# One shared inverse root for several output rows, and an early scaling of the second half's scan output in a free place

## The chip, the cores and the metric

The kernel runs on one core of a Trainium2 chip. The metric is the device time of one execution in microseconds (us); three runs of the kernel before gave 2174.93, 2175.2 and 2177.97 us, with a median of 2175.2 us.

## The reference

One decoder block over 1024 tokens of width 1024, all in float32. What matters here is the middle and the end: the scan branch ends in a norm over groups of 512 channels and a projection, the two branches are merged by gates, the merge is projected and added to the residual, and after the feed-forward network the residual is normed once more.

```python
y = ssd_chunked(xs, dt, A, Bm, Cm) + d_skip[:, None] * xs
y = y.reshape(b, S, 2048) * silu(z)
yg = y.reshape(b, S, 4, 512)
yg = yg * rsqrt(mean(yg * yg, -1) + EPS)          # one factor per token and group
y_ssm = (yg.reshape(b, S, 2048) * ssm_norm) @ w_ssm_out
...
mixed = gates[:, :, 0] * y_ssm + gates[:, :, 1] * y_att
x = x + mixed @ w_mix_out
h = rmsnorm(x, norm_ffn)
x = x + (silu(h @ w_ffn_gate) * (h @ w_ffn_up)) @ w_ffn_down
return rmsnorm(x, norm_final)
```

## The kernel before

A float32 product is made of three passes of a faster format: each operand is split into a high part (a cast on ScalarE) and a low part (operand minus high part, on VectorE), and `mm3` issues high x high, high x low and low x high. TensorE therefore needs, for every weight tile and every activation tile, one cast and one subtraction done before it.

The program is written out by a planner. `Pace` keeps a modelled clock `pace.t`, which advances with the matmuls that are issued. Everything else runs in generator tasks: a task that yields a list waits until the modelled time at which those buffers are written, a task that yields a string waits for an event, a number is a delay. The tasks fix the order of instructions in each engine's queue; on the chip each engine works through its queue in that order and waits on semaphores. All DMAs are issued from SyncE's queue (SP).

SBUF buffers are pieces of 4 KB per partition ("slabs") in a store; `slabs.room(n)` waits until n are free. `wts` is the store for weights: `w_dma` loads a raw weight tile, `w_split` makes the high and low tiles, `pump` (called by `tick` between matmuls) does both ahead of use as far as free pieces allow. `N_WTS` and `N_WTS_B` set how many pieces it has.

The stages that the change touches, in order:

- **Input projection.** The normalised rows `hhi`, `hlo` (both token halves in one tile each, 2 x 8 x 512) are the moving operands. After the last gate unit they are not read again.
- **Merge stage, first token half (`th` 0), then second (`th` 1).** `y_load` fetches the scan output of one half from DRAM in eight pieces `kk` (two 128-row blocks each) and two attention pieces, and per two pieces the norm's factor of each token, spread over partitions (`yscale`). `y_task` multiplies a piece by that factor on GpSimd (L1678), then casts it on ScalarE with the channel weight (L1689) and subtracts on VectorE (L1693), and fires `y{th}{kk}`. `mx_unit` (L1815) runs eight units of 60 matmuls over the pieces; `mx_task` (L1760) gates the result and writes it, split, into the half `th` 1 of `h2hi`, `h2lo`. Then `mix_unit` (L1845) multiplies by `w_mix_out` in two column blocks `cb`, four weight tiles `kp` each, and `mo_task` (L1775) adds the residual, forms the norm and writes the transposed rows of this half into `h2`. For `th` 0, `y_load(1)` and `y_task(1)` are started at the last unit (L1881), so that the second half's pieces are scaled and split while TensorE is in `mix_unit` of the first half. `lend` gives `W_MIX` slabs to `wts` for that time, `give_back` returns them.
- **End.** The down projection runs in seven products `PRODUCTS`; `down_out` (L2123) adds each result to the residual rows `xr`. When a half row (`b`) of one of the eight row tiles `jj` is complete, `out_half` (L2101) squares it on ScalarE with an accumulated sum and multiplies it by the norm's weight on GpSimd (L2108). With the second half row done, `inverse_root` (L2086) computes one row tile's factor on VectorE, 12 instructions on 128x1 operands, each of which needs the one before; then ScalarE scales the right half, VectorE the left half, and two DMAs write 256 KB each. Of `jj` 4 to 7 the left half (`b` 0) is the last to be done; it comes with the last product, one row tile after the other.

## Time and profile before

| | |
|---|---|
| median of 3 runs | 2175.2 us |
| the profiled execution | 2177.34 us |
| its span, first to last instruction | 2175.6 us |
| its mean granted TensorE clock | 0.993 |
| TensorE busy | 2129.2 us (98%) |
| VectorE busy | 1552.6 us (71%) |
| ScalarE busy | 907.9 us (42%) |
| GpSimd busy | 648.9 us (30%) |

TensorE is busy almost throughout, so a change in another engine's work moves the time only where TensorE waits for it, or where TensorE has already finished. Busy shares of the other engines are means over stages and say little; what counts is the few stretches in which TensorE has fewer matmuls than its full rate. Times in the rows below are us from the span's start. "DVE" is VectorE, "ACT" ScalarE, "POOL" GpSimd, "SPq" the queue of DMA issues, "PEld" the weight load of TensorE. All instructions carry the line of one helper (L169), so they are told apart by the names of their buffers; the number behind a name says which use of the buffer it is.

### The profile page before, as it was taken

What the parts mean: (1) busy time and instruction counts of PE and PEld (TensorE: products, weight loads), DVE (VectorE), ACT (ScalarE), POOL (GpSimd) and SP (SyncE); (2) the same over time, 40 slices, a digit from 0 to 9 for tenths busy, and PEclk for the clock granted to TensorE, in tenths of its full rate; (3) what the DMA queues carried; (4) which work ended last, traced back from release to release, by engine and by line L of the source; (5) the groups of instructions that cost most, each with busy time, mean ns of one, the idle gap of its engine ahead of it and who ended that gap; (6) DMA issues with size and microseconds to landing.
All of it is one profiled execution on the core that took longest, in us unless ns stands there. A gap on an engine that the chain in (4) does not pass through costs nothing. (4 is left out here: it accounts for less than half of the span.)

```text
span 2175.6 us, 27860 instructions
## 1 busy us (share of the span) xinstructions
PE 2129.2 (98%) x10356; PEld 1758.6 (81%) x10356; DVE 1552.6 (71%) x2124; ACT 907.9 (42%) x1642; POOL 648.9 (30%) x420
## 2 busy tenths in 40 slices
PE   6999999999999999999999999999999999999996
PEld 6788878888887888788888887888888888888885
DVE  6697887866656787897854347644897777767787
ACT  4543444344355565455533224322433332324444
POOL 1233222332114454454431004001254444420002
PEclk9999999999999999999999999999999999999998
DMA  3533343434364556675486467364143323349332
GB/s 129 167 97 107 106 126 103 119 104 126 102 206 158 176 190 200 214 233 172 128 259 210 133 195 235 118 187 131 41 139 99 111 82 116 107 161 356 98 97 102
DMA packets 308939, 322.90 MB, mean 148 GB/s; under 512 B 20740, under 2 KB 246980, under 8 KB 308548
## 3 DMA queue, kind: packets, MB, share of 16 engines
q1 hardware_dynamic: 308804, 321.13, 46.5%
q8 instruction: 81, 1.33, 0.3%
q14 instruction: 54, 0.44, 0.1%
HBM read 236.54 MB, written 84.54 MB: 148 GB/s over the span
## 5 line engine op out<-in xcount | busy, mean ns | idle before, releaser
L169 POOL TENSOR_TENSOR xr<-xr,nfin 128x512 f32<-128x512 f32 x16 | 21.8, 1369 | 185.1 <-ACT jk L169 185.1
L169 POOL TENSOR_TENSOR slab__8_12293<-h2hi,h2lo 128x1024 f32<-128x1024 f32 x1 | 2.7, 2723 | 117.5 <-PE wide__54_11935 L169 117.5
L169 POOL TENSOR_TENSOR slab__29_10800<-slab__29_10800,last__1_10783 128x1024 f32<-128x1024 f32 x1 | 2.4, 2391 | 115.8 <-DMA slab__29_10800<-yt_d 115.8
L169 POOL TENSOR_TENSOR slab__3_5034<-slab__3_5034,slab__3_5032 128x1024 f32<-128x1024 f32 x1 | 2.4, 2391 | 69.1 <-DMA slab__3_5032<-in_rope 69.1
L169 ACT ACTIVATE jk<-xr 128x512 f32<-128x512 f32 x16 | 10.1, 632 | 15.4 <-DVE xr L169 11.2
L169 POOL TENSOR_TENSOR slab__61_12556<-more__4_12496 128x512 f32<-128x512 f32 x1 | 1.3, 1290 | 49.8 <-DMA more__4_12496<-in_w_ffn_up 49.8
L169 POOL TENSOR_TENSOR slab__2_644<-slab__2_642 128x512 f32<-128x512 f32 x1 | 3.8, 3784 | 37.8 <-DMA slab__2_642<-in_w_in 37.8
L169 PE MATMUL wide__1_208<-hhi,slab__1_272 128*128 128x256 f32 (+1 forms) x24 | 8.8, 365 | 2.7 <-ACT hhi L169 2.7
L169 PE MATMUL wide__1_208<-hlo,slab__1_272 128*128 128x256 f32 (+1 forms) x24 | 8.9, 370 | 2.3 <-DVE hlo L169 2.3
L169 POOL TENSOR_TENSOR slab__16_12681<-slab__18_12618 128x512 f32<-128x512 f32 x1 | 2.8, 2823 | 27.6 <-DVE slab__15_12627 L169 27.6
L169 POOL TENSOR_TENSOR slab__45_15700<-slab__29_15392,slab__60_15513 128x512 f32<-128x512 f32 x1 | 1.3, 1300 | 32.1 <-DVE slab__60_15513 L169 32.1
L169 POOL TENSOR_TENSOR slab__14_10033<-slab__14_10033,slab__10_9841 128x1024 f32<-128x1024 f32 x1 | 3.0, 2978 | 26.2 <-DMA slab__14_10033<-yt_d 26.2
L169 POOL TENSOR_TENSOR slab__1_620<-hhi,hlo 128x1024 f32<-128x1024 f32 x1 | 2.4, 2407 | 26.9 <-DVE hlo L169 26.9
L169 ACT ACTIVATE xr<-xr,or 128x512 f32<-128x512 f32 x8 | 5.6, 717 | 11.3 <-DVE or L169 11.3
L169 DVE TENSOR_TENSOR hlo<-slab__1_624,hhi 128x1024 fp32r<-128x1024 f32 x1 | 1.2, 1224 | 11.8 <-DMA slab__3_906<-in_w_in 11.8
L169 DVE TENSOR_TENSOR slab__22_5025<-slab__19_4802,slab__19_5024 128x1024 fp32r<-128x1024 f32 x1 | 1.2, 1224 | 11.5 <-issue 11.5
L169 PE MATMUL wide__35_7344<-hhi,slab__25_7221 128*128 128x512 f32 x16 | 6.9, 431 | 1.7 <-DVE slab__6_7342 L169 1.7
L169 PE MATMUL bank__1_210<-ident 128*128 128x128 f32 x36 | 5.9, 343 | 2.7 <-DMA ident<-in_consts 2.7
L169 POOL TENSOR_TENSOR slab__9_9508<-slab__9_9508,slab__4_9506 128x1024 f32<-128x1024 f32 x1 | 2.4, 2403 | 20.0 <-DMA slab__9_9508<-yt_d 20.0
L169 PEld LDWEIGHTS wide__1_208<-hlo,slab__1_272 128*128 128x128 f32 x24 | 5.2, 217 | 3.9 <-DVE hlo L169 3.8
L169 PEld LDWEIGHTS wide__1_208<-hhi,slab__1_272 128*128 128x128 f32 x24 | 5.1, 213 | 4.0 <-ACT hhi L169 3.8
L169 PE MATMUL wide__1_208<-hhi,slab__1_273 128*128 128x256 f32 (+1 forms) x24 | 8.2, 343 | 0.0
(7956 smaller groups left out, 8285.8 us busy)
## 6 DMA issues: line engine op xcount, KB each, us to landing
xr<-x_d SPq DMA_DIRECT2D x8, 512.0 KB, 6.7
out<-xr SPq DMA_DIRECT2D x16, 256.0 KB, 2.4
b_d<-hhi SPq DMA_DIRECT2D x1, 1024.0 KB, 5.2
b_d<-hlo SPq DMA_DIRECT2D x1, 1024.0 KB, 7.3
slab__1_174<-in_x SPq DMA_DIRECT2D x1, 512.0 KB, 3.3
slab__1_175<-in_x SPq DMA_DIRECT2D x1, 512.0 KB, 4.9
slab__1_182<-in_norm_mix SPq DMA_DIRECT2D x1, 512.0 KB
slab__1_189<-in_w_in SPq DMA_DIRECT2D x1, 512.0 KB
```

The source lines that it names most:

```text
L169: r = call(*args, **kw)
```

## The change

Three things are changed.

- The factor multiplication of the second half's scan pieces is taken out of `y_load(1)`/`y_task(1)`. A new task `y1_scaled`, started when the last gate unit has been issued, loads the eight pieces into the place of the first half of `hhi`/`hlo`, one every 7 us of modelled time or later, and multiplies them on GpSimd there. To that end `hhi`, `hlo`, `h2hi` and `h2lo` become one tile per half; the first half of `h2` gets its place only when the pieces have been split (`yield "y17"` in `mo_task`). `y_task(1)` starts its splits after `mx07`, that is when the last unit of the first half has been gated.
- The weight store has 9 pieces instead of 7 in the merge stage, and borrows 1 slab instead of 4.
- At the end the sums of squares go to three groups of row tiles, 0 to 3, 4 alone, and 5 to 7, with one inverse root each on 128x4, 128x1 and 128x3 operands. The root has 14 instructions instead of 12. For `jj` above 3 and `b` 0 the norm's weight is no longer multiplied on GpSimd but in VectorE's final scaling.

The diff without the lines that only follow from the split of `hhi`, `hlo` and `h2` into halves:

```diff
-K_PAD, R_PAD = 40, 24
+K_PAD, R_PAD = 72, 24
...
-W_MIX = 4
+W_MIX = 1
...
+N_WTS_M = 9
...
+    def scale_rows(g, th, place):
+        yield from place.room()
+        t = yscale[th, g] = place.get([P, 512])
+        nc.sync.dma_start(t.v, rs_d[g].rearrange("c l -> (c l)")[th * 512:(th + 1) * 512].partition_broadcast(P))
+
+    def by_rows(raw, kk, th):
+        rsb = yscale[th, kk // 2]
+        yield [rsb, raw]
+        nc.gpsimd.tensor_tensor(raw.v, raw.v, rsb.v.unsqueeze(1).to_broadcast([P, 2, 512]), ALU.mult)
+        if kk % 2:
+            rsb.free()
+
+    def fetch_y(raw, kk, th):
+        g, f0 = kk // 2, (kk % 2) * 2
+        for i in range(2):
+            nc.sync.dma_start(raw.v[:, :, i * 256:(i + 1) * 256], yt_d[g][2 * th + i][:, f0:f0 + 2, :])
+
+    def y1_scaled():
+
+        for kk in range(8):
+            yield 7.0
+            yraw[1, kk] = Part(y1[kk // 4][:, kk % 4])
+            if kk % 2 == 0:
+                yield from scale_rows(kk // 2, 1, halves)
+            fetch_y(yraw[1, kk], kk, 1)
+            yield from by_rows(yraw[1, kk], kk, 1)
+            pace.fire(f"yr1{kk}")
+
     def y_load(th):
         ts_ = slice(th * 512, (th + 1) * 512)
-        for kk in range(10):
+        for kk in range(8 * th, 10):
...
     def y_task(th):
+        if th:
+            yield "mx07"
         for kk in range(10):
             yield f"yr{th}{kk}"
             raw = yraw[th, kk]
             yield [raw]
-            if kk < 8:
-                rsb = yscale[th, kk // 2]
-                yield [rsb]
-                nc.gpsimd.tensor_tensor(raw.v, raw.v, rsb.v.unsqueeze(1).to_broadcast([P, 2, 512]), ALU.mult)
-                if kk % 2:
-                    rsb.free()
+            if kk < 8 and th == 0:
+                yield from by_rows(raw, kk, th)
...
-    wts.pieces.extend(slabs.pieces.popleft() for _ in range(N_WTS - N_WTS_B))
+    wts.pieces.extend(slabs.pieces.popleft() for _ in range(N_WTS_M - N_WTS_B))
...
         if cb == 0:
             return
+        if th == 0:
+            yield "y17"
+            for n in ("hi", "lo"):
+                h2[n][0] = hp.tile([P, KD, 512], F32R, tag=f"h{n}0", name=f"h2{n}0")
...
-    h2["hi"] = hp.tile([P, 2, KD, 512], F32R, tag="hhi", name="h2hi")
-    h2["lo"] = hp.tile([P, 2, KD, 512], F32R, tag="hlo", name="h2lo")
+    y1 = [hp.tile([P, 4, 2, 512], F32, tag=f"h{n}0", name=f"y1{n}") for n in ("hi", "lo")]
+    for n in ("hi", "lo"):
+        h2[n] = [None, hp.tile([P, KD, 512], F32R, tag=f"h{n}1", name=f"h2{n}1")]
+    pace.spawn(y1_scaled(), 0.0, 1)
...
-    def inverse_root(v, r, t, sq):
-        nc.vector.tensor_scalar(v, sq[:, 0:1], sq[:, 1:2], D * EPS, ALU.add, ALU.add)
+    def inverse_root(v, r, t, h, sq):
+        nc.vector.tensor_tensor(v, sq[:, :, 0], sq[:, :, 1], ALU.add)
+        yield v
+        nc.vector.tensor_scalar(v, v, EPS, None, ALU.add)
         yield v
         nc.vector.tensor_scalar(t.bitcast(I32), v.bitcast(I32), 1, None, ALU.logical_shift_right)
+        nc.vector.tensor_scalar(h, v, -0.5, None, ALU.mult)
         yield t
         nc.vector.tensor_scalar(r.bitcast(I32), t.bitcast(I32), -1.0, 1597463007.0, ALU.mult, ALU.add)
         yield r
-        for c in (1.0, 1.0, D ** 0.5):
-            nc.vector.scalar_tensor_tensor(t, r, v, r, ALU.mult, ALU.mult)
+        for _ in range(3):
+            nc.vector.tensor_tensor(t, r, h, ALU.mult)
             yield t
-            nc.vector.tensor_scalar(t, t, -0.5 * c, 1.5 * c, ALU.mult, ALU.add)
+            nc.vector.tensor_tensor(t, t, r, ALU.mult)
             yield t
-            nc.vector.tensor_tensor(r, r, t, ALU.mult)
+            nc.vector.scalar_tensor_tensor(r, t, 1.5, r, ALU.add, ALU.mult)
             yield r
 
     def out_half(jj, b):
-        first = jj not in sums
-        if first:
-            sums[jj] = small("osq", 2)
+
+        group, n = ((0, 4), (4, 1), (5, 3))[(jj > 3) + (jj > 4)]
+        i = jj - group
+        if group not in sums:
+            sums[group] = [small("osq", 8)[:, :2 * n].rearrange("p (n b) -> p n b", b=2), 2 * n]
+        s = sums[group]
+        late = jj > 3 and b == 0
         xj = xr[:, jj, b * 512:(b + 1) * 512]
         yield [xr]
-        nc.scalar.activation(jk[:, b * 512:(b + 1) * 512], xj, AF.Square, accum_out=sums[jj][:, b:b + 1])
-        nc.gpsimd.tensor_tensor(xj, xj, nfin[:, b * 512:(b + 1) * 512], ALU.mult)
-        if first:
+        nc.scalar.activation(jk[:, b * 512:(b + 1) * 512], xj, AF.Square, scale=D ** -0.5, accum_out=s[0][:, i, b:b + 1])
+        if not late:
+            nc.gpsimd.tensor_tensor(xj, xj, nfin[:, b * 512:(b + 1) * 512], ALU.mult)
+        s[1] -= 1
+        if s[1]:
             return
-        v, r, t = (small(n, 1) for n in ("ov", "or", "ot"))
-        yield [sums[jj]]
-        for w in inverse_root(v, r, t, sums[jj]):
+        v, r, t, h = (small(k, 4)[:, :n] for k in ("rv", "rs", "rt", "sq"))
+        yield [s[0]]
+        for w in inverse_root(v, r, t, h, s[0]):
             if jj < 4:
                 yield [w]
-        xj = xr[:, jj, :]
-        rows = slice(jj * P, (jj + 1) * P)
-        nc.scalar.activation(xj[:, 512:], xj[:, 512:], AF.Copy, scale=r)
-        nc.vector.tensor_scalar(xj[:, :512], xj[:, :512], r, None, ALU.mult)
-        nc.sync.dma_start(out[rows, :512], xj[:, :512])
-        nc.sync.dma_start(out[rows, 512:], xj[:, 512:])
+        for i in range(n):
+            rows = slice((group + i) * P, (group + i + 1) * P)
+            xj, ri = xr[:, group + i, :], r[:, i:i + 1]
+            nc.scalar.activation(xj[:, 512:], xj[:, 512:], AF.Copy, scale=ri)
+            if late:
+                nc.vector.scalar_tensor_tensor(xj[:, :512], xj[:, :512], ri, nfin[:, :512], ALU.mult, ALU.mult)
+            else:
+                nc.vector.tensor_scalar(xj[:, :512], xj[:, :512], ri, None, ALU.mult)
+            nc.sync.dma_start(out[rows, :512], xj[:, :512])
+            nc.sync.dma_start(out[rows, 512:], xj[:, 512:])
```

## Rows read from the trace of the kernel before

**Rows 1.** The table by stage, in stretches of 50 us. Columns: the stretch and its length, busy us and instructions (x) of PE, PEld, DVE, ACT and POOL, granted clock of TensorE as a share of full speed, busy share of the DMA engines, GB/s.

```profile
1250.00:1300.00 50.00, 50.00 (x222) 41.40 (x221) 19.52 (x25) 11.84 (x14) 0.00 (x0) 1.00 0.61 188
1300.00:1350.00 50.00, 46.59 (x199) 38.08 (x198) 40.60 (x35) 23.55 (x36) 21.87 (x8) 0.97 0.74 246
```

**Rows 2.** The same table over three stretches cut at the stages' own borders: the eight units of the first half, the last stretch with matmuls, and what follows the last matmul.

```profile
1203.00:1311.70 108.70, 108.70 (x482) 90.02 (x481) 43.12 (x52) 27.86 (x36) 4.88 (x3) 1.00 0.57 176
...
2100.00:2159.00 59.00, 58.50 (x256) 47.45 (x254) 49.69 (x122) 28.66 (x59) 13.33 (x11) 1.00 0.24 76
2159.00:2175.60 16.60, 0.03 (x1) 0.00 (x0) 10.11 (x44) 4.11 (x7) 2.37 (x2) 0.64 0.47 176
```

**Rows 3.** The waits of TensorE: what it was about to write, what released it; total us, times, longest.

```profile
PE bank__136_10900 L169 <- DVE slab__34_10952 L169: 3.4, 1, 3.4
...
PE bank__170_17092 L169 <- DVE slab__43_17287 L169: 0.5, 1, 0.5
```

**Rows 4.** The timeline of TensorE around that longest wait: the first matmul of the first half's mix, the last matmul ahead of the wait, and the one behind it (start us, us).

```profile
1311.69 0.39 PE L169 MATMUL bank__136_10900<-slab__27_10854,h2hi 128*128 128x512 f32 x1
...
1322.57 0.39 PE L169 MATMUL bank__136_10900<-slab__46_10951,h2hi 128*128 128x512 f32 x1
1326.37 0.50 PE L169 MATMUL bank__136_10900<-slab__34_10952,h2hi 128*128 128x512 f32 x1 [3.41 <-DVE slab__34_10952 L169]
```

**Rows 5.** The table by stage over the time right behind that wait (columns as in rows 1).

```profile
1326.37:1333.35 6.98, 6.98 (x24) 5.59 (x25) 6.89 (x6) 3.20 (x4) 2.19 (x1) 0.76 0.01 2
```

**Rows 6.** The timeline of VectorE in the same stretch: the subtractions of the second half's scan pieces (two SBUF inputs and "par"), the gating of the last unit (slab__10, input from PSUM in the first row of it), the weight subtraction that TensorE waits for (slab__34_10952), and a scan piece's subtraction later on.

```profile
1309.27 5.70 DVE L169 SCALAR_TENSOR_TENSOR slab__36_10850<-slab__29_10800,par,slab__35_10849 128x512 fp32r<-128x512 f32 x2 [3.33 <-ACT slab__35_10849 L169]
...
1316.03 1.27 DVE L169 SCALAR_TENSOR_TENSOR slab__10_10723<-slab__10_10723,wide__49_10782 128x512 f32<-128x512 f32 x2
1317.34 1.58 DVE L169 TENSOR_TENSOR slab__10_10723<-slab__10_10723 128x512 f32<-128x512 f32 x1
1318.85 3.56 DVE L169 SCALAR_TENSOR_TENSOR slab__14_10887<-slab__29_10812,par,slab__11_10886 128x512 fp32r<-128x512 f32 x2
1322.33 2.85 DVE L169 TENSOR_TENSOR h2lo<-slab__10_10723,h2hi 128x512 fp32r<-128x512 f32 x1
1325.10 1.21 DVE L169 TENSOR_TENSOR slab__34_10952<-slab__38_10837,slab__46_10951 128x1024 fp32r<-128x1024 f32 x1
...
1332.14 1.41 DVE L169 SCALAR_TENSOR_TENSOR slab__12_10978<-slab__28_10879,par,slab__29_10977 128x512 fp32r<-128x512 f32 x2
```

**Rows 7.** The timeline of GpSimd there: three of the eight multiplications of the second half's scan pieces.

```profile
1306.09 2.39 POOL L169 TENSOR_TENSOR slab__29_10800<-slab__29_10800,last__1_10783 128x1024 f32<-128x1024 f32 x1 [115.79 <-DMA slab__29_10800<-yt_d]
...
1315.56 2.82 POOL L169 TENSOR_TENSOR slab__28_10879<-slab__28_10879,last__1_10815 128x1024 f32<-128x1024 f32 x1 [1.14 <-DMA slab__28_10879<-yt_d]
...
1321.96 2.67 POOL L169 TENSOR_TENSOR slab__3_10979<-slab__3_10979,last__2_10932 128x1024 f32<-128x1024 f32 x1
```

**Rows 8.** The timeline of ScalarE and SP there: the cast of the weight tile that TensorE waits for, and the DMA issues of that tile and of the first scan piece of the second half.

```profile
1319.48 1.05 ACT L169 CAST slab__46_10951<-slab__38_10837 128x1024 fp32r<-128x1024 f32 x1
```

```profile
1299.83 0.75 SPq L169 DMA_DIRECT2D slab__29_10800<-yt_d  x1
...
1304.60 0.48 SPq L169 DMA_DIRECT2D slab__38_10837<-in_w_mix_out  x1
```

**Rows 9.** The chain that ended last, one piece of it: the first unit of the second half.

```profile
1360.88 13.94 PE wide__50_11248 L169 x60
```

**Rows 10.** The timelines at the border between the last two units of the first half: VectorE's low part of the last unit's first weight tile, and of its second; TensorE's first matmul of that unit, and its first one with that low part.

```profile
1295.80 1.23 DVE L169 TENSOR_TENSOR slab__45_10771<-slab__45_10736,slab__45_10770 128x1024 fp32r<-128x1024 f32 x1 [6.76 <-ACT slab__45_10770 L169]
...
1300.22 1.22 DVE L169 TENSOR_TENSOR slab__45_10795<-slab__37_10762,slab__46_10794 128x1024 fp32r<-128x1024 f32 x1
```

```profile
1298.09 0.39 PE L169 MATMUL wide__49_10782<-slab__26_9568,slab__45_10770 128*128 128x512 f32 x1
...
1298.54 0.39 PE L169 MATMUL wide__49_10782<-slab__26_9568,slab__45_10771 128*128 128x512 f32 x1
```

**Rows 11.** The timeline of the end: the last addition to the residual, the last square and the read of its sum, a root that starts (ov) and the scaling that follows it, and the last scalings of ScalarE and VectorE.

```profile
2159.06 0.69 DVE L169 SCALAR_TENSOR_TENSOR xr<-bank__181_17095,xr 128x512 f32<-128x512 f32 x1 [1.18 <-PE bank__181_17095 L169]
...
2160.39 0.18 ACT L169 ACTIVATION_READ_ACCUMULATOR jk<-xr 128x1 f32 x1
...
2164.16 0.21 DVE L169 TENSOR_SCALAR ov<-osq 128x1 f32<-128x1 f32 x1
...
2166.76 0.48 DVE L169 TENSOR_SCALAR xr<-xr,or 128x512 f32<-128x512 f32 x1
...
2169.82 1.33 ACT L169 ACTIVATE xr<-xr,or 128x512 f32<-128x512 f32 x2 [2.35 <-DVE or L169]
2169.83 0.88 DVE L169 TENSOR_SCALAR xr<-xr,or 128x512 f32<-128x512 f32 x2
```

**Rows 12.** VectorE from 2100 to 2176, grouped by operation and form (count | busy us, mean ns): the longest of the roots' small instructions, the final scaling, and an addition that has, as the new final scaling has, two 128x512 inputs.

```profile
L169 DVE SCALAR_TENSOR_TENSOR ot<-or,ov 128x1 f32<-128x1 f32 x24 | 7.0, 292 | 0.5
...
L169 DVE TENSOR_SCALAR xr<-xr,or 128x512 f32<-128x512 f32 x8 | 4.0, 505 | 0.4
...
L169 DVE SCALAR_TENSOR_TENSOR xr<-bank__181_17095,xr 128x512 f32<-128x512 f32 x1 | 0.7, 692 | 1.2 <-PE bank__181_17095 L169 1.2
```

**Rows 13.** The DMA view from 2140 to 2180 in 40 slices of 1 us: the row of GB/s, and the group of the output's DMAs with the median us from issue to landing.

```profile
GB/s 0 0 0 0 0 0 0 0 0 0 0 256 268 0 0 0 14 371 373 283 16 262 262 0 0 367 158 0 338 186 0 309 383 356 0 0 0 0 0 0
...
out<-xr SPq DMA_DIRECT2D x16, 256.0 KB, 2.4
```

More of the change, by code (lines that the diff above doesn't have):

```diff
@@ L146, in _key @@
         if name.startswith(big) and hasattr(a, "offset"):
-            return f"{big}.{part(a.offset)}"
+            return f"{name.split('__')[0]}.{part(a.offset)}"
     return name.split("__")[0]
@@ L485, in hybrid_block @@
     ysum = kpool.tile([P, NG, NCH], F32, name="ysum")
-    hhi = hp.tile([P, 2, KD, 512], F32R, tag="hhi", name="hhi")
-    hlo = hp.tile([P, 2, KD, 512], F32R, tag="hlo", name="hlo")
+    hhi, hlo = ([hp.tile([P, KD, 512], F32R, tag=f"{n}{th}", name=f"{n}{th}") for th in range(2)] for n in ("hhi", "hlo"))
     hp.tile([P, R_PAD], F32, name="hpad")
@@ L594, in t_rest @@
             for q in range(2):
-                t4, hi, lo = (T["T4"][q],) + tuple(a[:, 1, q * 2:q * 2 + 2, :] for a in (self.hi, self.lo))
+                t4, hi, lo = (T["T4"][q],) + tuple(a[1][:, q * 2:q * 2 + 2, :] for a in (self.hi, self.lo))
                 nc.scalar.copy(hi, t4.v)
@@ L978, in dt_task @@
             for k in range(KD):
-                mm(ps.v, wd[:, k, :], hhi[:, th, k, :], k == 0, False)
-                mm(ps.v, wd[:, k, :], hlo[:, th, k, :], False, k == KD - 1)
+                mm(ps.v, wd[:, k, :], hhi[th][:, k, :], k == 0, False)
+                mm(ps.v, wd[:, k, :], hlo[th][:, k, :], False, k == KD - 1)
             yield [ps]
@@ L1446, in tile_task @@
         yield [xt]
-        yield from split_tokens(xt.v, hhi[:, 0], hlo[:, 0], i * P)
+        yield from split_tokens(xt.v, hhi[0], hlo[0], i * P)
         pace.fire(f"h{i}")
@@ L1562, in save_b12 @@
         for d, h in zip(b12_d, (hhi, hlo)):
-            nc.sync.dma_start(d, h[:, 1, :4, :].bitcast(F32))
+            nc.sync.dma_start(d, h[1][:, :4, :].bitcast(F32))
     b12 = []
@@ L1641, in spare, with __init__, free @@
             yield 0.5
+    class Part:
+        def __init__(self, v):
+            self.v = v
+        def free(self):
+            pass
+    def scale_rows(g, th, place):
[21 more added lines that the diff above has]
+            pace.fire(f"yr1{kk}")
     def y_load(th):
         ts_ = slice(th * 512, (th + 1) * 512)
-        for kk in range(10):
+        for kk in range(8 * th, 10):
             if kk > 2:
                 yield f"y{th}{kk - 3}"
-            g, f0 = kk // 2, (kk % 2) * 2
+            g = kk // 2
             for ev in (f"ssd{g}",) if kk < 8 else (f"sl{kk * 2 - 16}", f"sl{kk * 2 - 15}"):
@@ L1656, in y_load @@
             if kk < 8 and kk % 2 == 0:
-                place = slabs if th == 0 else halves
-                yield from place.room()
-                yscale[th, g] = place.get([P, 512])
-                nc.sync.dma_start(yscale[th, g].v, rs_d[g].rearrange("c l -> (c l)")[ts_].partition_broadcast(P))
+                yield from scale_rows(g, th, slabs)
             yield from slabs.room()
             raw = yraw[th, kk] = slabs.get([P, 2, 512])
-            for i in range(2):
-                if kk < 8:
-                    nc.sync.dma_start(raw.v[:, :, i * 256:(i + 1) * 256], yt_d[g][2 * th + i][:, f0:f0 + 2, :])
-                else:
+            if kk < 8:
+                fetch_y(raw, kk, th)
+            else:
+                for i in range(2):
                     nc.sync.dma_start(raw.v[:, i, :], att_d[(kk - 8) * 2 + i][:, ts_])
@@ L1807, in mo_task @@
             yield [xj]
-            yield from split_tokens(xj, h2["hi"][:, th], h2["lo"][:, th], j * P, raw)
+            yield from split_tokens(xj, h2["hi"][th], h2["lo"][th], j * P, raw)
             x2t[th, j].free()
```

32 lines of the change are left out of this document (16 added, 16 removed).

## The prediction

> **What bounds the kernel now.** I read the table by stage first. TensorE is the bound: at its full rate a stretch of 50 us holds 222 matmuls, one per 0.227 us at a granted clock of 1.00 [rows 1], and nearly all stretches from 100 us on hold that. So a gain can only lie where a stretch has fewer, or behind the last matmul. Two places that the change touches show that. The stretch from 1300 to 1350 us holds 199 matmuls at clock 0.97, which is 23 x 0.227 = 5.2 us less work than its neighbour; and behind 2159 us no matmul runs for 16.6 us, with VectorE busy for 10.1 of them [rows 1, 2].
>
> **The place at 1300.** The waits of TensorE, read next, name one long wait, for a VectorE result, 3.4 us [rows 3]. In the timeline, the mix of the first half begins at 1311.69; its third weight tile is due at 1322.57, and the low part of that tile (slab__34_10952) is the operand on which TensorE stands until 1326.37 [rows 4]. Issue to issue that is 3.80 us where 0.23 are normal: 3.57 lost. Right behind it 24 matmuls take 6.98 us at a granted clock of 0.76, where full rate gives 5.44: another 1.54 lost, part of the time at the lower level of 1.2 instead of 2.4 GHz after a pause of 3.4 us [rows 4, 5]. Together 5.1 us, which agrees with the 5.2 from the count.
>
> Why was that low part late? Its cast was done at 1320.5 [rows 8]; the subtraction began at 1325.10. Ahead of it in VectorE's queue stand two pairs of scan pieces' subtractions and the last unit's gating, and they are stretched: a pair takes 5.70 and 3.56 us where a later pair takes 1.41, and a 512-wide subtraction with both inputs in SBUF takes 2.85 [rows 6]. All the stretched ones lie beside GpSimd's multiplications of 2.4 to 2.8 us each; the gating's first row, whose input is in PSUM, runs beside one of them and takes 1.27 for two, unstretched [rows 6, 7]. So the wait is made by VectorE and GpSimd standing in each other's way in this stretch.
>
> **Part 1: the early scaling.** It removes eight multiplications, their four factor loads and sixteen piece loads from this stretch, and holds the pieces' casts and subtractions back until the last unit is gated. The gating's own chain from the end of unit 7 (1311.7) is 1.27 + about 0.7 + a cast of 0.6 + the planned 0.7 + 0.7, so `mx07` comes near 1316. With pairs at 1.41 instead of 5.70 and 3.56, and none of them ahead of the gating, the third tile's low part is free 4.3 + 2.2 us sooner than now, and 3.8 would do. I take the whole 5.1 us; the bounds are 0 (another instruction is last) and 5.2.
>
> What starts later? The second half's unit begins at 1360.88 [rows 9] and uses one piece every 1.36 us. Eight pieces from 1316 on need 8 x 1.41 = 11.3 us of VectorE, which has 45 us until then and besides them some 8 weight subtractions of 1.2 us and eight residual additions of 0.7, 15 us in all. So they are in time with about 18 us to spare; behind them `y17` comes before 1360, and the rows that wait for it in `mo_task` are not used by TensorE before the feed-forward stage. Cost nothing; if the cover went, each piece would cost its lateness.
>
> What moves ahead: eight multiplications, and on SP four factor loads and sixteen piece loads, go into the first half's units, from 1210 us on. There VectorE is busy 43 of 108.7 us, DMA 57%, and TensorE has no gap [rows 2]. SP queues the weight loads of the units behind these DMAs; they wait for the gate units' last read of the place, which 7 us of delay should cover. From issue to multiplication took 6.3 us in the crowded stretch [rows 7, 8]; with the delay of 7 and a multiplication of 2.8 a step is at most 16 us, 8 x 16 = 129 us, so by 1339 at the latest, and near 1300 if the load takes half of that. Their price is the stretching of the units' weight subtractions. The tightest is the first of a unit: finished at 1297.03, used at 1298.54, 1.5 us of slack; the next was done at 1301.44 and due 2.5 us later [rows 10], by eight steps of 0.68 us from the unit's start. A multiplication that begins just ahead of it can hold it 2.8 us, 1.3 past the slack. Against that, two more weight pieces let one more tile be split ahead, which adds some 5 us of slack. I take 0, with bounds 0 and 8 x (1.3 + 1.5 for the clock) = 22 us.
>
> On this mechanism the Trainium skill (page "SBUF — State Buffer", section "Who interferes with whom") says that a VectorE instruction with two SBUF inputs contends with a GpSimd instruction that reads SBUF, and that the one that comes second is blocked for the whole of the first, not slowed. The trace agrees with the first half (2.85 us with two SBUF inputs, 0.64 each with one in PSUM). By it, the multiplications are not made cheaper by being moved: each can still block one subtraction wholly, which is the slower rival below.
>
> The weight store with 9 pieces and one lent slab (10 in the mix, before 11) neither adds nor removes an operation; the other stages' small waits, of 0.1 to 0.4 us, I leave as they are. The padding moves addresses; no row prices that, I take 0.
>
> **Part 2: the end.** Now: the last addition begins at 2159.06, its square's sum is read by 2160.57, then VectorE computes the roots of three rows after each other; one, from its first instruction to the scaling behind it, takes 2166.76 - 2164.16 = 2.60 us, 0.217 per instruction. The last scaling ends at 2171.15, and the span ends 4.45 us later, at 2175.6 [rows 11]. In these 4.45 us four DMAs of 256 KB flow, at 309 to 383 GB/s [rows 13].
>
> After: the root of three rows starts at the same 2160.57. Its width (3 instead of 1) costs nothing at these sizes; of its 14 instructions one (`h`) needs no predecessor's result, so 13 x 0.217 = 2.8 us, to 2163.4. Then ScalarE scales three right halves (0.72 and twice 0.61: 1.33 for two [rows 11]) and VectorE three left halves with two inputs, 0.69 each by the addition of that form where the old scaling took 0.505 [rows 12]: ready from 2164.1, the last at 2165.4. Six DMAs, 1.57 MB, follow. Bounds: if ends follow the last scaling as now, 2165.4 + 4.45 = 2169.9, a gain of 5.7. If the DMAs are the limit: flow from 0.7 us behind the first ready half, 2164.8, at 370 GB/s 4.25 us, at the single DMAs' 262 GB/s 6.0 us [rows 13], then 1.6 us to the end as now (flow ended near 2174): 2170.7 or 2172.4, gains of 4.9 or 3.2. I take 4.8, near the rate that four DMAs in a row had.
>
> Row 4 keeps a root of its own, which ends before the last addition as now. Rows 0 to 3 share one: three roots, 36 instructions of 0.15 to 0.29 us [rows 12], leave VectorE's queue between 2125 and 2160, where TensorE waits 0.5 us for a subtraction [rows 2, 3]; but four scalings of 0.505 come in a burst, perhaps ahead of the last subtractions. Bounds +0.5 and -2.0; I take +0.2. The four GpSimd multiplications that go (`b` 0) had stretched single root instructions in the tail; that is inside the 4.8.
>
> **Sum.** 5.1 + 0 + 4.8 + 0.2 = 10.1 us. Against its own time the profiled execution would go from 2177.3 to 2167.2 (span 2175.6 to 2165.5). It stands 2.1 us above the median of the three runs, which I take as the base: 2175.2 - 10.1 = **2165.1 us**.
>
> **The rivals.**
> - *The wait at 1322 moves instead of going* (0.17). The weight tile is held by ScalarE's order: its cast came only at 1319.48, behind the gating's cast [rows 8], and if the planner puts the split of that tile behind pieces again, TensorE stops as long. For: the tile's load was issued at 1304.60, 15 us before its cast. Against: with 1.41 per pair there are 5 us left. Only the end gains: 2175.2 - 5.0 = 2170.2.
> - *The end is bound by its DMAs or by the burst of scalings* (0.09): the gain there is 3.2 - 2.0, with the mix's 5.1 some 6.3 in all: 2168.9. For: single pairs flowed at 262 GB/s. Against: three and four in a row did 356 to 383.
> - *The moved multiplications stop TensorE in the first half's units* (0.07), the one that ends slower. Place: the first weight subtraction of each unit. Price: 1.3 us of wait and 1.5 of clock behind it, 2.8 per hit. From four hits in eight on, 11.2 us, the gain of 10.1 is gone; with six, 16.8: 2175.2 - 10.1 + 16.8 = 2181.9. For: 1.5 us of slack [rows 10]. Against: a multiplication of 2.8 us covers this subtraction by chance only in about (2.8 + 1.2)/13.6 of the cases, 0.3, two or three of eight, and the deeper store hides those.
> - *The change doesn't do what it says* (0.05): the multiplications slide into the mix again, and the rows' burst eats the root's gain: within 4 us of 2175.2.
>
> **How the numbers follow.** The forecast gets 0.62: 2165.1, by its bounds 2162.5 (5.2, 5.7, 0.5 and some 1.3 of other small waits gained by the deeper weight store) to 2168. The first two rivals lie at 2168.9 and 2170.2, so a range of 2162 to 2171.5 leaves out the last two cases and little of the others. A difference of 0.2%, about what a measurement of this kernel can tell from no change, is 4.35 us. Faster by more: 0.62 + 0.08 + 0.12 = 0.82 (the first rival at 5.0 is close to the bound). Same: 0.11. Slower: 0.07.
>
> **What would show it.** Right: 220 or more matmuls between 1300 and 1350 at clock 1.00, no wait of over 1 us for a weight's low part; the eight multiplications on GpSimd between 1210 and 1311; pairs of 1.4 us on VectorE behind 1316; a gap of 11 to 12 us instead of 16.6 behind the last matmul with one root in it, and six output DMAs in a row at 350 GB/s or more. Wrong: waits of TensorE in the first half's units on weights (1203 to 1311.7), or in the second half's first unit on scan pieces; output DMAs that begin later than 2165 on this clock; an end that stays though the root is short.

## The result and the profile after

The changed kernel takes 2166.46 us (median of 5 runs, 2166.28 to 2167.63), the kernel before, run beside it, 2177.97 us (2174.93 to 2179.6). The ratio is 0.9946 with a 95% interval from 0.9935 to 0.9958: faster by 0.54%. The profiled executions have spans of 2164.7 and 2175.6 us. Cut at the same matmuls in both traces, the 10.9 us between them lie here:

| stretch | before, us | after, us | difference |
|---|---|---|---|
| start of the last gate unit | 1192.01 | 1192.62 | +0.6 |
| from there to the first half's mix | 119.68 | 120.51 | +0.8 |
| mix of the first half | 49.19 | 43.86 | -5.3 |
| eight units of the second half | 113.54 | 112.66 | -0.9 |
| its mix, feed-forward, down projection, to the last matmul | 684.60 | 683.57 | -1.0 |
| behind the last matmul | 16.58 | 11.48 | -5.1 |

The spans are known to 0.1 us, so a time behind the last matmul holds to 0.05 us. The first row is no effect of the change: over all kernels below this start lies between 1190.4 and 1195.3 us. Differences of 1 us in a whole time can come from there alone, so below the stretches are compared as well as the times.

The table by stage after (columns as in rows 1) answers to [rows 1, 2]:

```profile
1250.00:1300.00 50.00, 49.48 (x219) 40.58 (x218) 20.77 (x23) 11.27 (x14) 7.20 (x3) 1.00 0.73 225
1300.00:1350.00 50.00, 50.00 (x222) 41.44 (x221) 36.72 (x41) 25.31 (x39) 5.24 (x2) 1.00 0.52 169
1203.00:1313.10 110.10, 109.58 (x483) 90.36 (x483) 47.60 (x52) 27.42 (x34) 17.26 (x7) 1.00 0.64 196
```

The stretch from 1300 on now holds the full 222 matmuls at clock 1.00, and GpSimd has 5.24 us of work in it where it had 21.87. The first half's units have VectorE busy for 47.6 us instead of 43.1, GpSimd for 17.3 instead of 4.9, and TensorE, which had no gap there, has one of 0.5 us. Of the waits of TensorE in the merge stage this one is new, and that of [rows 3] is gone:

```profile
PE wide__48_10724 L170 <- DVE slab__43_10748 L170: 0.5, 1, 0.5
```

The timeline ahead of this wait shows a moved multiplication on GpSimd, a subtraction of the gating on VectorE beside it, and two casts on ScalarE:

```profile
1285.82 2.40 POOL L170 TENSOR_TENSOR y1lo<-y1lo,last__2_10608 128x1024 f32<-128x1024 f32 x1 [11.55 <-DMA y1lo<-yt_d]
1286.62 2.15 DVE L170 TENSOR_TENSOR slab__16_10563<-slab__16_10563 128x512 f32<-128x512 f32 x1
1288.81 0.62 ACT L170 CAST h2hi<-slab__16_10563 128x512 fp32r<-128x512 f32 x1 [10.79 <-DVE slab__16_10563 L170]
1289.33 1.04 ACT L170 CAST slab__45_10747<-slab__34_10676 128x1024 fp32r<-128x1024 f32 x1
```

The subtraction takes 2.15 us where it takes 0.69 alone. The cast of the gated rows waits for it, the cast of the weight stands behind that cast, and the weight's low part (slab__43_10748) comes late.

The timeline of VectorE in the first half's mix (from 1313.13) answers to [rows 6], that of GpSimd to [rows 7]:

```profile
1313.33 1.28 DVE L170 SCALAR_TENSOR_TENSOR slab__17_10752<-slab__17_10752,wide__49_10812 128x512 f32<-128x512 f32 x2 [2.71 <-PE wide__49_10812 L170]
...
1315.26 1.22 DVE L170 TENSOR_TENSOR slab__37_10921<-slab__43_10856,slab__45_10920 128x1024 fp32r<-128x1024 f32 x1
1316.39 0.68 DVE L170 TENSOR_TENSOR h2lo<-slab__17_10752,h2hi 128x512 fp32r<-128x512 f32 x1
1318.21 3.27 DVE L170 TENSOR_TENSOR slab__44_10951<-slab__44_10891,slab__13_10950 128x1024 fp32r<-128x1024 f32 x1 [1.14 <-ACT slab__13_10950 L170]
1321.41 1.40 DVE L170 SCALAR_TENSOR_TENSOR slab__29_10941<-y1hi,par,slab__27_10940 128x512 fp32r<-128x512 f32 x2
```

```profile
1214.44 2.41 POOL L170 TENSOR_TENSOR y1hi<-y1hi,last__1_10223 128x1024 f32<-128x1024 f32 x1 [23.55 <-PE wide__45_10171 L170]
...
1306.70 2.85 POOL L170 TENSOR_TENSOR y1lo<-y1lo,last__2_10828 128x1024 f32<-128x1024 f32 x1 [18.47 <-DMA y1lo<-yt_d]
1318.01 2.39 POOL L170 TENSOR_TENSOR y1lo<-y1lo,last__2_10828 128x1024 f32<-128x1024 f32 x1 [8.46 <-DMA y1lo<-yt_d]
```

The third weight tile's low part (slab__37_10921) is done at 1316.5 and first used at 1324.2; before, it came 3.4 us after TensorE stopped for it. The gating ends at 1317.1 and the pairs behind it take 1.40. Seven of the eight multiplications lie in the units; the eighth, at 1318.01, still falls into the mix and stretches a weight subtraction from 1.22 to 3.27 us, which nobody waits for.

The end, on VectorE (answers to [rows 11]), and the DMA view's row of GB/s in 40 slices of 1 us from 2130 on (answers to [rows 13]):

```profile
2153.26 0.69 DVE L170 SCALAR_TENSOR_TENSOR xr<-bank__181_17087,xr 128x512 f32<-128x512 f32 x1 [1.51 <-PE bank__181_17087 L170]
2154.80 0.16 DVE L170 TENSOR_TENSOR rv<-osq 128x3 f32<-128x3 f32 x1 [0.85 <-ACT jk L170]
...
2157.17 0.16 DVE L170 SCALAR_TENSOR_TENSOR rs<-rt,rs 128x3 f32<-128x3 f32 x1
2157.37 2.08 DVE L170 SCALAR_TENSOR_TENSOR xr<-xr,rs,nfin 128x512 f32<-128x512 f32 x3
```

```profile
GB/s 12 229 29 0 0 0 0 0 0 0 0 0 0 0 0 0 0 262 371 383 373 391 371 391 80 0 0 0 10 371 385 379 385 43 0 0 0 0 0 0
```

One root of 2.57 us for three rows, then three scalings, and the last six DMAs flow from 2159 to 2163.1 without a gap at about 380 GB/s; the span ends 1.6 us later.

### The profile page after: what moved, and what is told of

Read it like the earlier page. It is cut to its first block, busy times and chain, and to the rows that moved or that the text cites. A ratio compares the mean times of both kernels' runs of the same rounds, so it can differ in the third digit from the quotient of the medians.

```text
span 2164.7 us, 27768 instructions
## 1 busy us (share of the span) xinstructions
PE 2127.4 (98%) x10356; PEld 1759.1 (81%) x10356; DVE 1541.9 (71%) x2070; ACT 907.8 (42%) x1642; POOL 641.4 (30%) x416
## 4 chain that ended last, share of the span: by engine, by line
PE 91%; DVE 5%; ACT 2%; issue 1%; DMA 0%; SPq 0%; DVEq 0%; ACTq 0%
PE wide__60_16859 L170 1%; PE wide__59_16858 L170 1%; PE wide__59_16409 L170 1%; PE wide__58_16408 L170 1%; PE wide__58_15921 L170 1%; PE wide__57_15920 L170 1%; PE wide__50_11253 L170 1%; PE wide__51_11366 L170 1%; PE wide__48_10626 L170 1%; PE wide__51_11496 L170 1%; PE wide__54_11935 L170 1%; PE wide__53_11848 L170 1%; PE wide__53_11753 L170 1%; PE wide__52_11666 L170 1%; PE wide__52_11579 L170 1%
## 5 line engine op out<-in xcount | busy, mean ns | idle before, releaser
L170 POOL TENSOR_TENSOR xr<-xr,nfin 128x512 f32<-128x512 f32 x12 | 17.3, 1451 | 172.1 <-ACT jk L170 171.7
L170 POOL TENSOR_TENSOR slab__3_5036<-slab__3_5036,slab__3_5034 128x1024 f32<-128x1024 f32 x1 | 2.4, 2396 | 69.5 <-DMA slab__3_5034<-in_rope 69.5
L170 ACT ACTIVATE jk<-xr 128x512 f32<-128x512 f32 x16 | 10.1, 634 | 16.6 <-DVE xr L170 16.5
L170 POOL TENSOR_TENSOR y1hi<-y1hi,last__1_10223 128x1024 f32<-128x1024 f32 x2 | 4.8, 2407 | 37.0 <-PE wide__45_10171 L170 23.6
L170 POOL TENSOR_TENSOR y1lo<-y1lo,last__2_10828 128x1024 f32<-128x1024 f32 x2 | 5.2, 2620 | 26.9 <-DMA y1lo<-yt_d 26.9
L170 PE MATMUL wide__1_210<-hhi,slab__1_274 128*128 128x256 f32 (+1 forms) x24 | 8.9, 371 | 4.0 <-ACT hhi L170 4.0
L170 POOL TENSOR_TENSOR y1lo<-y1lo,last__2_10608 128x1024 f32<-128x1024 f32 x2 | 4.8, 2398 | 24.0 <-DMA y1lo<-yt_d 24.0
L170 POOL TENSOR_TENSOR y1hi<-y1hi,last__1_10418 128x1024 f32<-128x1024 f32 x2 | 4.8, 2400 | 21.9 <-DMA y1hi<-yt_d 21.9
L170 POOL TENSOR_TENSOR slab__32_10035<-slab__32_10035,slab__10_9843 128x1024 f32<-128x1024 f32 x1 | 2.4, 2396 | 27.1 <-DMA slab__32_10035<-yt_d 27.1
L170 DVE TENSOR_TENSOR hlo<-slab__1_626,hhi 128x1024 fp32r<-128x1024 f32 x1 | 1.2, 1224 | 11.9 <-DMA slab__3_908<-in_w_in 11.9
L170 DVE TENSOR_TENSOR slab__22_5027<-slab__19_4804,slab__19_5026 128x1024 fp32r<-128x1024 f32 x1 | 1.2, 1224 | 11.5 <-issue 11.5
L170 PEld LDWEIGHTS bank__1_212<-ident 128*128 128x128 f32 x36 | 6.4, 199 | 2.6 <-DMA ident<-in_consts 2.6
```

The costliest lines, as they stand in the source:

```text
L170: r = call(*args, **kw)
```

## The experiments

Ratios are to the kernel before as it was run beside each, with 95% intervals; medians of different rows were not all taken side by side, so the ratios are what to compare. "To the mix" is the time from the last gate unit to the first half's mix, "to the last matmul" that from the second half's mix on, "gap" that behind the last matmul.

| kernel | median, us | ratio | to the mix, us | to the last matmul, us | gap, us |
|---|---|---|---|---|---|
| before | | 1 | 119.68 | 684.60 | 16.58 |
| after | 2166.46 | 0.9946 (0.9935 to 0.9958) | 120.51 | 683.57 | 11.48 |
| end alone | 2172.42 | 0.9974 (0.9965 to 0.9983) | 120.06 | 683.53 | 11.42 |
| merge alone | 2171.93 | 0.9977 (0.9969 to 0.9986) | 119.68 | 684.58 | 16.58 |
| early order | 2166.18 | 0.9952 (0.9936 to 0.9967) | 120.34 | 683.53 | 11.42 |
| before, held back | 2173.42 | 0.9983 (0.9974 to 0.9992) | 119.68 | 684.64 | 16.50 |
| before, on VectorE | 2174.98 | 0.9986 (0.9977 to 0.9995) | 120.21 | 684.59 | 16.50 |
| end and hold-back | 2168.18 | 0.9960 (0.9947 to 0.9974) | 119.78 | 683.55 | 11.49 |
| old store | 2177.47 | 1.0004 (0.9995 to 1.0013) | 130.76 | 683.59 | 11.46 |
| weight on GpSimd | 2166.69 | 0.9954 (0.9939 to 0.9969) | 121.27 | 683.54 | 12.76 |
| own roots | 2169.92 | 0.9965 (0.9952 to 0.9977) | 119.68 | 683.53 | 14.07 |
| group of four | 2167.70 | 0.9954 (0.9937 to 0.9972) | 119.68 | 683.52 | 12.78 |
| own roots first | 2170.53 | 0.9965 (0.9953 to 0.9978) | 119.68 | 684.30 | 14.32 |
| pairs | 2164.97 | 0.9944 (0.9927 to 0.9961) | 119.69 | 683.56 | 11.85 |

### Each part alone

"End alone" is the kernel before with the new `inverse_root`, `out_half` and padding:

> The kernel before with the shared roots and the late weight in VectorE's scaling alone; the merge stage as before. If the two parts add up: the gap behind the last matmul is 11.5 us (16.6 before), the last matmul comes 0.5 to 1.0 us earlier by what VectorE no longer does between 2100 and 2160, 5.6 to 6.1 us gained in all, ratio 0.9972 to 0.9975; the stretch 1300 to 1350 keeps its 199 matmuls and the wait of 3.4 us. Rival: the early last matmul of the changed kernel came from the merge part; then the gap alone is gained, 5.1 us, ratio 0.9977.

"Merge alone" is the changed kernel with the old ones:

```diff
-K_PAD, R_PAD = 72, 24
+K_PAD, R_PAD = 40, 24
-    (new inverse_root, out_half)
+    (inverse_root, out_half of the kernel before)
```

> The changed kernel with the end as before (a root for each row, weight on GpSimd). If the parts add up: the first half's mix takes 44 us instead of 49.2, the units of the first half lose 0.5 to 0.8 us to one late weight part, 4.5 to 5 us gained, ratio 0.9977 to 0.9980; the gap behind the last matmul is 16 to 16.8 us. Rival: the ends depend on each other (a different phase at the end), then the gap differs from 16.6 by over 1 us.

The parts add: 0.9974 x 0.9977 = 0.9951, inside the interval of the whole. With the end alone the wait at the third weight tile stays (3.0 us), and the 1.0 us ahead of the last matmul is gained; with the merge alone neither end term is. So the 1.0 us belongs to the end's part.

### What made the wait: order or contention

Three kernels take one of the two things away. The first ("early order") lets the pieces' subtractions go as early as they did before the change, with the multiplications moved:

```diff
     def y_task(th):
-        if th:
-            yield "mx07"
```

> The changed kernel, but the second half's splits don't wait for the gating of the first half's last unit; the early multiplications stay. Theory A (VectorE's subtractions were late because GpSimd's multiplications stretched them): no wait of over 1 us in the first half's mix, which takes 44 to 44.5 us; time within 0.05% of the changed kernel, ratio about 0.9946. Theory B (they were late because the pieces' subtractions stood ahead of the gating and the weight in VectorE's queue, stretched or not): a wait of 2 to 3.5 us on a weight's low part or on the gated rows comes back, mix 46 to 49 us, ratio 0.9958 to 0.9970.

The second ("before, held back") holds the subtractions of the kernel before back, and leaves its multiplications on GpSimd in the mix:

```diff
     def y_task(th):
+        if th:
+            yield "mx07"
```

> The kernel before, with the second half's pieces held back until the first half's last unit is gated, multiplications on GpSimd and all; nothing else. Theory B (order): the gating and the weight come first, the wait of 3.4 us goes, mix 44 to 45 us, ratio 0.9977 to 0.9985 unless the pieces are late for the second half's first unit. Theory A (contention): the same multiplications now lie beside the later weight subtractions, waits of 2 to 5 us in the mix or at the second half's first pieces, ratio 0.9990 to 1.0020.

The third ("before, on VectorE") leaves the order of the kernel before and gives the second half's eight multiplications to VectorE:

```diff
-                nc.gpsimd.tensor_tensor(raw.v, raw.v, rsb.v.unsqueeze(1)
+                (nc.vector if th else nc.gpsimd).tensor_tensor(raw.v, raw.v, rsb.v.unsqueeze(1)
```

> The kernel before with the second half's eight multiplications on VectorE instead of GpSimd, in the same place in the order. Theory A (the stretching by GpSimd is a needed part of the wait): four multiplications of 1.2 us come ahead of the third weight tile's low part, 4.9 us, but 9.5 us of stretching go; the wait of 3.4 us goes, the mix takes 44 to 45 us, ratio 0.9977 to 0.9985. Theory B (VectorE's order and load alone): the wait stays at 2 to 5 us, ratio 0.9995 to 1.0010.

The wait at the third weight tile is gone in all three. (Later in the merge stage the first has a new wait of 0.5 us and the third one of 1.3.) VectorE in the second kernel, with the gating, two pairs of pieces and the third tile's low part (slab__34_10942, first used at 1324.7):

```profile
1315.13 1.84 DVE L169 TENSOR_TENSOR slab__10_10723<-slab__10_10723 128x512 f32<-128x512 f32 x1
1317.66 0.69 DVE L169 TENSOR_TENSOR h2lo<-slab__10_10723,h2hi 128x512 fp32r<-128x512 f32 x1 [0.69 <-ACT h2hi L169]
1318.29 3.57 DVE L169 SCALAR_TENSOR_TENSOR slab__36_10916<-slab__29_10800,par,slab__35_10915 128x512 fp32r<-128x512 f32 x2
1321.78 1.21 DVE L169 TENSOR_TENSOR slab__34_10942<-slab__38_10837,slab__46_10941 128x1024 fp32r<-128x1024 f32 x1
1322.92 3.55 DVE L169 SCALAR_TENSOR_TENSOR slab__11_10929<-slab__29_10812,par,slab__28_10928 128x512 fp32r<-128x512 f32 x2
```

The pairs are still stretched, but only one stands ahead of the tile, which is done at 1323.0, 1.7 us ahead of its use. And in the third kernel a piece's pair and a multiplication stand between gating and tile, all unstretched, and the tile is done earlier still:

```profile
1313.37 0.69 DVE L169 TENSOR_TENSOR slab__10_10723<-slab__10_10723 128x512 f32<-128x512 f32 x1
1313.98 1.41 DVE L169 SCALAR_TENSOR_TENSOR slab__14_10887<-slab__29_10812,par,slab__11_10886 128x512 fp32r<-128x512 f32 x2
1315.31 1.22 DVE L169 TENSOR_TENSOR slab__30_10817<-slab__30_10817,last__1_10815 128x1024 f32<-128x1024 f32 x1
1316.44 0.68 DVE L169 TENSOR_TENSOR h2lo<-slab__10_10723,h2hi 128x512 fp32r<-128x512 f32 x1
1317.05 1.22 DVE L169 TENSOR_TENSOR slab__34_10952<-slab__38_10837,slab__46_10951 128x1024 fp32r<-128x1024 f32 x1
```

So neither theory stands alone. The wait needed both: pieces queued ahead of the tile, and GpSimd stretching them. Removing either is enough, and in each of the three runs the theory that expected a remaining wait missed. That makes the early scaling dispensable for this gain, which the next kernel tries: the kernel before with the new end and the two lines that hold the splits back.

> The kernel before with two changes: the new end, and the second half's pieces held back until the first half's last unit is gated, with the multiplications left in the mix on GpSimd and the weight store as before. If holding back does what the early scaling does, the parts add: ratio 0.9974 x 0.9983 = 0.9957 by the two runs, or, by the traces' own stages (6.15 us at the end, 5.3 + 0.65 in the merge stage), 12.1 us, ratio 0.9944. If the early scaling is worth something of its own, the time is over 1 us above the changed kernel.

It has no wait at the tile, and its stretches are those of the changed kernel to within 0.8 us. Its profiled span is 2165.2 us, after's 2164.7. Its median is 1.7 us above that of the changed kernel, over the 1 us that the expectation named as a sign that the early scaling is worth something, but the intervals of the two ratios overlap: no run here tells the two apart.

### The rival that ends slower: the store as it was

```diff
-W_MIX = 1
+W_MIX = 4
-N_WTS_M = 9
+N_WTS_M = 7
```

> The changed kernel with 7 weight pieces in the merge stage and 4 lent in the mix, as before. Theory (the deeper store hides the moved multiplications): each multiplication that lands on a unit's first weight subtraction now costs up to 2.8 us, two or three of eight do, so the first half's units take 3 to 8 us more than in the kernel before (0.8 in the changed one), ratio 0.9960 to 0.9985. Rival (the store is idle, the slack of 1.5 us is enough): 0 to 1 us, ratio 0.9943 to 0.9950. The mix has no wait of over 1 us under either.

The whole gain is gone. The mix and the end are as in the changed kernel, but up to the mix it takes 11.1 us more than the kernel before, where the expectation had 3 to 8. One row of the table by stage, the two longest waits of TensorE there, and the timeline of SP, ScalarE, VectorE and TensorE ahead of the longest:

```profile
1250.00:1300.00 50.00, 47.02 (x190) 36.26 (x191) 23.21 (x25) 9.71 (x12) 10.60 (x4) 0.97 0.63 191
```

```profile
PE wide__47_10442 L170 <- ACT slab__39_10436 L170: 1.3, 1, 1.3
PE wide__48_10624 L170 <- ACT slab__42_10618 L170: 0.8, 1, 0.8
```

```profile
1241.04 0.38 SPq L170 DMA_DIRECT2D slab__39_10388<-in_w_ssm_out  x1
1241.47 0.57 SPq L170 DMA_DIRECT2D last__1_10406<-rs_d  x1
1242.10 2.52 SPq L170 DMA_DIRECT2D y1hi<-yt_d  x2
...
1247.76 1.04 ACT L170 CAST slab__39_10436<-slab__39_10388 128x1024 fp32r<-128x1024 f32 x1 [7.59 <-DMA slab__39_10388<-in_w_ssm_out]
1248.84 1.23 DVE L170 TENSOR_TENSOR slab__44_10437<-slab__39_10388,slab__39_10436 128x1024 fp32r<-128x1024 f32 x1 [7.95 <-ACT slab__39_10436 L170]
...
1248.86 0.50 PE L170 MATMUL wide__47_10442<-slab__26_9570,slab__39_10436 128*128 128x512 f32 x1 [1.34 <-ACT slab__39_10436 L170]
```

Nine waits add up to 5.2 us; the rest of the 11.1 is matmuls that follow each other more slowly, right behind the waits above all (190 in 50 us, clock 0.97). The longest wait is not made by a multiplication that holds a subtraction: the next one begins at 1249.72, after the wait. None of the nine casts and subtractions that TensorE waited for is stretched (1.04 to 1.05 us a cast, 1.22 to 1.23 a subtraction). Six of the waits, 3.8 us, are for a unit's first weight, whose cast waited for its load; the other three, 1.4 us, come behind a gating's subtraction that a multiplication stretches from 0.69 to 2.83 and to 2.18 us, as in the changed kernel. So the theory has the sign and the store right, but not the way in which most of the time is lost. ScalarE stood idle for 7.6 us until the weight tile had landed, 6.7 us after its issue, with a factor load and two piece loads issued right behind it. In the trace of before the tile in this place was cast 5.3 us after its issue (1235.49 to 1240.78), in that of after 11.3 (1224.90 to 1236.16): with two more pieces the load is issued 19.4 us ahead of the unit's start instead of 8.2, most of a unit earlier. So place and sign of the prediction's slower rival were right, and what is late here is above all the load. That the loads issued together slow each other fits, but no run took the piece loads away alone.

### The end

The norm's weight on GpSimd for all rows again (`late = False`):

> The changed kernel with the norm's weight multiplied on GpSimd for all rows, the shared roots stay. Theory (the shared root is the gain, the folding little): the last row's multiplication ends before the root does, single root instructions are stretched by 0.5 to 0.8 us, each left half is scaled 0.2 us faster; the gap behind the last matmul is 11.4 to 12.3 us (11.5 in the changed kernel). Rival (the multiplication on GpSimd was on the path): 13 us or more.

The root takes 4.1 us instead of 2.57, since its first two instructions run beside GpSimd's three multiplications, busy from 2154.11 to 2157.8:

```profile
2156.02 0.60 DVE L170 TENSOR_TENSOR rv<-osq 128x3 f32<-128x3 f32 x1 [0.85 <-ACT jk L170]
2156.66 1.19 DVE L170 TENSOR_SCALAR rv<-rv 128x3 f32<-128x3 f32 x1
2157.89 0.17 DVE L170 TENSOR_SCALAR rt<-rv 128x3 int32<-128x3 int32 x1
```

Folding the weight into the last scaling is worth 1.3 us of the gap (12.76 against 11.48), which lies between what the theory (up to 12.3) and the rival (13 or more) expected.

A root for each of rows 4 to 7, weight folded as in the changed kernel (`(0, 4) if jj < 4 else (jj, 1)`):

> The changed kernel with a root for each of the rows 5, 6 and 7; rows 0 to 3 share one as in the changed kernel, and the norm's weight stays in VectorE's scaling. Theory (two roots of 2.6 to 2.7 us went from the path): the gap behind the last matmul is 15 to 16.5 us instead of 11.5, ratio 0.9964 to 0.9972. Rival (the roots were hidden by the output's DMAs): under 13 us.

With a gap of 14.07 sharing is worth 2.6 us; the expected 15 to 16.5 was too much. VectorE works the three roots off one after the other, 3.17 us each with its scaling:

```profile
2155.37 0.75 DVE L170 SCALAR_TENSOR_TENSOR xr<-xr,rs,nfin 128x512 f32<-128x512 f32 x1
...
2158.54 0.75 DVE L170 SCALAR_TENSOR_TENSOR xr<-xr,rs,nfin 128x512 f32<-128x512 f32 x1
...
2161.71 0.75 DVE L170 SCALAR_TENSOR_TENSOR xr<-xr,rs,nfin 128x512 f32<-128x512 f32 x1
```

The roots are as serial as expected, but when the last is done only two DMAs are left, and the span ends 3.8 us behind the last scaling's end.

Rows 4 to 7 in one group, so that eight DMAs follow the root instead of six (`((0, 4), (4, 4))[jj > 3]`):

> The changed kernel with rows 4 to 7 in one group of four. One root less, but eight DMAs at the end instead of six. Theory (behind the shared root the end is bound by the DMAs, 0.69 us each): the gap grows by 1.4 us to 12.9. Rival (bound by the last scaling): by one scaling of 0.6 us to 12.1, or less.

The gap is 1.30 us longer than after's for two more DMAs, 0.65 each. At 380 GB/s a DMA of 262 kB is 0.69 us. One more scaling alone would have made it 0.6. So behind a shared root the end is bound by its DMAs.

Roots of their own for rows 0 to 3 (`(jj, 1) if jj < 5 else (5, 3)`):

> The changed kernel with a root of its own for each of the rows 0 to 3; rows 4 and 5 to 7 as in the changed kernel. Theory (what VectorE no longer does between 2120 and 2150 brings the last matmul forward): the time from the feed-forward stage's start to the end of the last matmul grows from 659.1 to 659.6 to 660.2 us (660.1 in the kernel before), the gap stays at 11.5 us. Rival: the last matmul came earlier for the late rows' sake; then it stays at 659.1.

TensorE waits again ahead of the last matmul, 0.4 us, and that stretch is 0.7 us longer than in the changed kernel; but the gap is 14.32 where 11.5 was expected. The DMA row, in 40 slices of 0.75 us from 2130, and ScalarE's last scalings:

```profile
GB/s 229 14 8 0 0 0 0 0 0 0 0 0 0 0 0 14 375 135 0 168 356 0 0 0 250 283 0 53 385 381 379 385 383 379 277 0 0 0 0 0
...
out<-xr SPq DMA_DIRECT2D x16, 256.0 KB, 2.6
```

```profile
2156.29 3.31 ACT L170 ACTIVATE xr<-xr,rs 128x512 f32<-128x512 f32 x5 [2.05 <-DVE rs L170]
```

Five scalings and not three: two rows of the first four are still open when the last root begins, and their DMAs join the burst. Four more at 0.69 would make 11.48 + 2.76 = 14.24.

Last, whether fewer DMAs behind the last root make the kernel faster: groups 0 to 3, 4 and 5, 6 and 7.

> The kernel after with the groups of row tiles 0 to 3, 4 and 5, 6 and 7 at the end; nothing else. Theory (behind the shared root the end is bound by the output's DMAs, about 0.69 us each, of which six follow the last root in the kernel after): four follow it, and the gap behind the last matmul goes from 11.48 to 11.48 - 2 x 0.69 = 10.1 us; the span ends 1.4 us sooner, a ratio to the kernel before of about 0.994, which the intervals hardly tell from 0.9946, so the gap in the trace decides. Rival (the root of rows 4 and 5 is issued as one block, and the last two rows' additions wait behind it on VectorE): the last addition and the root behind it come up to 2.6 us later, and the gap is 11.5 to 12.7 us.

The interval of the ratio does not tell it from the changed kernel. Its profiled span of 2162.0 is shorter because its last gate unit began at 1190.41; the gap is 11.85, not 10.1. VectorE shows why:

```profile
2148.07 0.15 DVE L170 TENSOR_TENSOR rv<-osq 128x2 f32<-128x2 f32 x1
...
2150.64 1.42 DVE L170 SCALAR_TENSOR_TENSOR xr<-xr,rs,nfin 128x512 f32<-128x512 f32 x2
2151.97 0.68 DVE L170 SCALAR_TENSOR_TENSOR xr<-bank__181_17087,xr 128x512 f32<-128x512 f32 x1
```

The last matmul ends at 2150.15, but the last addition stands behind the root and the scalings of rows 4 and 5 until 2151.97, 1.8 us; in the changed kernel it begins 0.04 us behind the last matmul. Two DMAs fewer give 1.4 back: 11.48 + 1.8 - 1.4 = 11.9. The rival was right.

## Why the prediction was right, point by point

It said 2165.1 us with a range from 2162.0 to 2171.5; 2166.46 was measured. Its gain of 10.1 us stands against 10.9 between the spans; its base of 2175.2 was the median of three runs where five now give 2177.97. So the base was 2.8 us too low and the gain too small (11.5 between the medians): that the forecast comes within 1.4 us of the time is partly luck, as the two offset each other.

- *The place at 1300, 5.1 us:* 5.3 were gained, in the mix, as it said. The loss was rightly read as wait and slow clock behind it. The reason was half right: it named contention and order together and took the gain for both at once, under the early scaling, but a hold-back of two lines gets the same with the contention left in.
- *The moved multiplications, 0:* +0.8 us up to the mix, in which the one named wait of 0.5 lies. It depends on who starts first in one place. In the changed kernel and in "weight on GpSimd", with the same merge stage, and in "early order", the multiplication begins ahead of the gating's subtraction (by 0.80, 0.03 and 0.98 us), which then takes 2.15, 2.91 and 1.96 us, and 0.8, 1.6 and 0.7 us are lost up to the mix. In merge alone, own roots, group of four, own roots first and pairs, all with the same merge stage, it begins 0.04 to 0.7 us behind the subtraction's start; that takes 0.69 us, and nothing is lost, though now the weight's subtraction behind it is the stretched one (1.7 to 1.9 us). So what the slower rival feared does happen, but it costs time at the gating and not at a unit's first weight, and less than 2.8 a hit. The eight come in steps of 11 to 21 us, so that the last is at 1318, between the prediction's "near 1300" and its bound of 1339. The reason given for taking 0, the deeper store, is what the run with the old store confirms: without it the term is 11.1. The rival's price of 2.8 per hit came from stretched subtractions, while in that run six of nine waits were for a late load and three came behind the stretched gating. The "some 5 us" of slack that the deeper store adds were right: the low part of the first weight of the unit at 1244.30 is done at 1238.4 and used at 1244.75, 6.3 us where [rows 10] had 1.5.
- *Second half's pieces, 0:* no wait for a piece; the units even took 0.9 us less. 0.6 of that is a unit of the kernel before with a wait of 0.3 us for a weight, which the end alone, with the merge stage of before, does not have either (112.92 us for its units); so it is no effect of the pieces.
- *The end, 4.8 us:* 5.1. The root measured 2.57 us against 2.8, six DMAs flowed in 4.1 us against 4.25 and the span ended 1.6 us behind, as put. By the experiments 2.6 belong to sharing and 1.3 to the folded weight; the effects overlap, so the two need not add up to the whole. The bound with 6.0 us of flow, and with it the second rival, rest on a misreading of [rows 13]: 256 and 268 are one pair of DMAs, 524 KB, cut by the border of two slices of 1 us. In slices of 0.1 us the same pair flows at 348 to 451 GB/s in the slices that it fills, as fast as four in a row.
- *VectorE ahead of the last matmul, 0.2 us:* this term was mis-sized; 1.0 was gained. TensorE's wait of 0.5 [rows 3] was only half of it: the same 12 matmuls of that row tile took 3.66 us before (2147.02 to 2150.68) and 2.72 after (2142.18 to 2144.90). Roots of their own for rows 0 to 3 lose 0.7 of it again. The feared burst of four scalings costs nothing.

## What to carry to other kernels

When a queue holds what the bound engine needs behind what nobody needs yet, ask first for the order: holding the unneeded work back cost two lines here and gave the same 5 us as moving eight multiplications into another stage. Loads and multiplications moved into a full stage cost little here (0 to 1.6 us) only together with a deeper weight store, with which that stage's own loads are issued earlier; that store was worth 11 us. At the end of a kernel count both the serial steps and the DMAs behind the last one (0.65 to 0.69 us each here), and do not put a finished row's root ahead of the last row's addition in the same queue.

## What the hardware showed that was not expected

- The subtraction at 1318.21 took 3.27 us beside a multiplication that ran until 1320.40: 2.19 us until it ended and 1.08 behind it, about the 1.22 that it takes alone. And where the gating's subtraction started first, by 0.04 to 0.3 us in four of the runs, it took its 0.69 and the multiplication 2.7 to 2.9 instead of 2.4. That is blocking and not sharing, as the Trainium skill has it for two SBUF inputs (page "SBUF — State Buffer", section "Who interferes with whom").
- But a root instruction with one tensor input, 128x3, took 1.19 us instead of 0.17 beside GpSimd, and ended (2157.85) with its multiplications (2157.82). Small operands do not protect from it.
- The width of the small instructions costs 0.02 us at most: in the changed kernel's last two roots 0.16 to 0.17 us on 128x3 and 0.14 to 0.16 on 128x1, and 0.195 from one to the next that needs it.
- Six to ten DMAs of 256 KB in a row flowed at 371 to 387 GB/s in full slices. The pairs with pauses around them in the trace before are no slower while they flow: the 256 and 268 of [rows 13] are means of slices that a pair fills only in part.
